# Hybrid encoder layer on one core: whole loads at the start, two steps in halves at the end, and a token tile finished by a transfer

## The chip, the core and the metric

The kernel runs on one core of a Trainium2 chip. The core has TensorE (matmuls; PE in the profile, its weight loads PEld), VectorE (DVE), ScalarE (ACT), GpSimd (POOL) and SyncE (SP), which work side by side and wait for each other by semaphores. Transfers between HBM and the on-chip memory are issued from SP, ACT or POOL and move by 16 DMA engines. POOL can also issue a transfer that adds what it carries to what stands at its destination. The metric is the device time of the kernel in microseconds.

## The reference

One layer of a hybrid streaming encoder in fp32, batch 1, 512 tokens, model width 1024, recurrent width 1280, 16 attention heads, feed-forward width 3072:

```python
h = rms_norm(x, mix_norm_pre)
proj = h @ w_in                       # -> xa, ga, q, k, v, f_logit, g_a, g_b
xc = causal_dwconv(xa, conv_a_w, conv_a_b)
hr = rg_lru(xc, w_rg_a, b_rg_a, w_rg_x, b_rg_x, lru_lambda)
y_a = gelu(ga) * hr
y_b = forgetting_attention(q, k, v, f_logit + b_forget)
merged = sigmoid(g_a + b_merge[0]) * (y_a @ w_proj_a) + sigmoid(g_b + b_merge[1]) * (y_b @ w_proj_b)
x = x + rms_norm(merged @ w_out, mix_norm_post)
h = rms_norm(x, ffn_norm_pre)
up = causal_dwconv(h @ w_up, conv_f_w, conv_f_b)
gate, val = split(up)
x = x + rms_norm((gelu(gate) * val) @ w_down, ffn_norm_post)
```

`rms_norm` divides a token's row by the root of its mean square and multiplies by a gain. So nothing of a token can be scaled before its whole row of 1024 is there.

## The kernel before, in words

Every product is made of three matmuls: each fp32 operand is split into a high and a low part, and high by high, high by low and low by high are summed in a PSUM bank. The high part is a cast on ScalarE (`wh`, `hh`, `ah`; line 172 for a weight), the low part a subtraction, mostly on VectorE (`wl`, line 175). A weight tile is 128x1024 fp32, 512 KB, and comes by a transfer on SP's queue (`raw`, line 166). In part of the stages the weight's low part is made without VectorE: ScalarE writes minus the high part (line 361), and POOL issues a transfer that adds the raw weight to it (line 362).

The stages follow each other on TensorE: the norm of x and the first four `xa` units (to about 36 us), the rest of the input projection with the recurrent branch (to 235), the two merge gates `ma` and `mb` (235 to 335), attention (to 480), the projections and `wo` (to 540), the second norm and the first `up` units (to 590), the `up` units in pairs (to 790), and the `down` product with the last norm.

The order within each stage is partly written out by hand (`manual_schedule`: instructions stand on an engine in the order of the code), partly set by the framework's scheduler, which may move an instruction where its inputs and buffers allow; `issue_after` holds an instruction behind another one.

The prologue (lines 557 to 676) is written out by hand. x comes in four token tiles of 128 tokens (`xt`), tiles 0 and 1 in halves of 512 columns. For each tile ScalarE makes the sum of squares (`sumsq` by halves with an addition on VectorE for tiles 0 and 1, `sumsq_whole` for 2 and 3) and the root, VectorE the reciprocal (`rs`) and the scaling by the gain (`scaled`, line 616), TensorE turns the 128x128 blocks (`turn`, line 245), ScalarE casts the result into `hh` (`evac_hi`, line 249), and VectorE makes `hl` (`evac_lo`). The gain is first spread over all partitions by four matmuls against ones (line 595). `spin(n)` are n matmuls whose result nobody reads, in the bank of `xa3`. `X` is the first half of the 512 tokens (tiles 0 and 1), `Y` the second. The first four `xa` units are done in halves, X of all four and then Y of all four (`half`, which issues 24 matmuls of 256 columns).

The gates and the `up` pairs use a Strassen-like scheme (`Halved`, `Pair`): two units share seven products of sums of quarters. `period` runs a pair `p` together with the finishing of the pair before it and the preparation of the two behind. The parts that need a plain weight quarter come by `plain_low` and `plain_high`, in index 0 for a whole tile (128x1024) and index 1 for half a tile.

The second norm (`mix_norm`, a generator that is run in pieces) makes `x2t`, the residual stream, and its scaled rows `xn`, which are turned (`tr_f`, line 260) for the `up` product. While tiles 2 and 3 of it are under way, TensorE does the first halves of some `up` units (`first_half`), and `fetch` loads and splits the weights ahead of them.

The `down` product has seven products of six steps each (`STEPS`), into banks `dn`. The last one is product 2, for token tiles 0 and 1; its last four steps (`LATE`) are held back and run per token tile, tile 1 in two column halves with a bank each, so that the norm of the first half can begin early. At the end `fold_part` adds the bank into `kept` and squares it, `gained_part` multiplies by the gain, `scale_of` makes the reciprocal root (`rs_o`), and the result is finished in one of two ways:

```python
def finish(t, c, queue):
    dve.scalar_tensor_tensor(out=os[t][:, c], in0=os[t][:, c], scalar=rso[t], in1=x2t[:, t, c],
                             op0=ALU.mult, op1=ALU.add)
    queue.dma_start(ov[:, t, c], os[t][:, c])

def finish_by_dma(t, queue):
    act.activation(out=os[t], in_=os[t], func=AF.Copy, scale=rso[t])
    nc.gpsimd.dma_start(os[t], x2t[:, t], accum_op=ALU.add)
    queue.dma_start(ov[:, t], os[t])
```

Tiles 2 and 3, which are ready while TensorE still works, take `finish_by_dma` (2 with its store on POOL, 3 on SP). Tiles 0 and 1 take `finish`.

Of the kernel before, what the change touches and what calls it, by code (L numbers as in the profile page):

```python
# [63 lines left out]
def kernel(  # L64
# [267 lines left out]
    class Halved:  # L332


        def __init__(self, prefix, block, xh, xl):
            self.prefix, self.block, self.xh, self.xl = prefix, block, xh, xl
            self.sh = self.sl = self.tpool = self.kpool = self.stpools = None

    class Pair:


        def __init__(self, st, j, tiles):
# [4 lines left out]
            self.w, self.t, self.th, self.x, self.ml = {}, {}, {}, {}, {}  # L347

# [18 lines left out]
        def plain_high(self, i):  # L367
# [75 lines left out]
    def period(p, b, n1, n2, epilogue, load):  # L443
# [22 lines left out]
        n2.plain_low(0)  # L466
# [19 lines left out]
    with ExitStack() as rg:  # L486
        rt, ixt, tt = {}, {}, {}
        last_act = [None]
        with ExitStack() as r0:
# [68 lines left out]
            with tc.tile_pool(name="pre", bufs=2, side="right", reuse_waits="tile") as pre, ExitStack() as wp:  # L558
                offset(wp, 256, "right")
                wpre = wp.enter_context(tc.tile_pool(name="wpre", bufs=3, side="right", reuse_waits="tile"))  # L560
# [14 lines left out]
                us += [Split(*order[t][1:], order[t][0], (wpre, None)[t - 2]) for t in range(2, NF)]  # L575
# [14 lines left out]
                for i, c in enumerate(HALVES):  # L590
# [8 lines left out]
                def sumsq(t):  # L599
                    xns[t] = pre.tile([P, D], F32, tag="xn", name=f"xn{t}")  # L600
                    s2 = small.tile([P, 2], F32, tag="s2", name=f"s2_p{t}")
                    for i, c in enumerate(HALVES):
                        act.activation(out=xns[t][:, c], in_=xts[t][:, c], func=AF.Square, accum_out=s2[:, i : i + 1])
                    ss = small.tile([P, 1], F32, tag="ss", name=f"ss_p{t}")
                    dve.tensor_tensor(out=ss, in0=s2[:, 0:1], in1=s2[:, 1:2], op=ALU.add)
                    rss[t] = rstd_of(ss, f"p{t}")
# [24 lines left out]
                sumsq(0)  # L631
# [18 lines left out]
                wh, wl = us[0].parts()  # L650
                for w, h in ((wh, hh), (wh, hl), (wl, hh)):
                    for k in range(KD):
                        pe.matmul(pss[0][:, X], w[:, k], h[:, k, X], start=w is wh and h is hh and k == 0, stop=w is wl and k == KD - 1)
# [7 lines left out]
                scaled(3, 1)  # L661
                us[2].hi()
# [250 lines left out]
    with ExitStack() as g2:  # L913
# [14 lines left out]
        gates.stpools = [st0pool, st1pool]  # L928
        none = Nothing()
# [239 lines left out]
    turned = {}  # L1169
    with ExitStack() as mix:  # L1170
# [12 lines left out]
        def mix_norm(t, acc):  # L1183
# [21 lines left out]
            for c in HALVES:  # L1205
                dve.scalar_tensor_tensor(out=xn[:, c], in0=x2t[:, t, c], scalar=rs, in1=gb[1][:, c],
                                         op0=ALU.mult, op1=ALU.mult)
# [60 lines left out]
        fetch(where[f"up{1 + JF}"])  # L1268
        first_half(1)
        next(g2)  # L1270
        next(g3)
# [125 lines left out]
    wd, yraw, yhl, dpools, LATE = {}, {}, {}, [], 4  # L1397
# [339 lines left out]
```

## Time and profile before

| what | value |
|---|---|
| median of the three runs shown | 912.75 us (912.56 to 912.94) |
| profiled execution, device time | 912.11 us |
| its span (first to last instruction) | 910.3 us |
| granted clock of TensorE, mean | 0.998 |
| TensorE busy | 900.5 us |
| VectorE, ScalarE, POOL busy | 728.1, 601.6, 219.5 us |
| moved by transfers | 187.86 MB, mean 206 GB/s |

The profile belongs to one execution. Its device time is 1.8 us longer than its span, and differences between two kernels are taken between like numbers. A row of a timeline reads: start in us, duration, engine, line, operation, output <- inputs, shapes, how many instructions, and in brackets the idle time ahead of it with the engine, tile and line that ended it. A row of the chain has the start, the duration and what carried it. Matmuls overlap: one of 256 columns is listed with 0.28 us, but they start 0.12 us apart, and the step from start to start is its price.

### The profile page before, as it was taken

Reading aid. Unit: us, or ns where it says so; the run is one execution under the profiler, and the core shown is the slowest. Engines: PE = TensorE matmul, PEld = TensorE weight load, DVE = VectorE, ACT = ScalarE, POOL = GpSimd, SP = SyncE. Lnnn points to the kernel's source line nnn. Section 1 sums busy time; section 2 is a strip of 40 time slices with the busy share of each in tenths; the row PEclk is TensorE's granted clock in tenths of the full one; section 3 lists DMA queues with packets and bytes.
Section 4 is the critical chain, followed back from the end, with each engine's and each line's share of the span. In section 5 each row is a group of like instructions: output and inputs, shape, how many; then the busy total and the mean of one; then the engine's idle time right before and its main releaser. Section 6 shows DMA issues by size and latency. Waiting matters only on the chain.

```text
span 910.3 us, 15947 instructions
## 1 busy us (share of the span) xinstructions
PE 900.5 (99%) x5906; PEld 803.4 (88%) x5906; DVE 728.1 (80%) x1201; ACT 601.6 (66%) x1041; POOL 219.5 (24%) x281
## 2 busy tenths in 40 slices
PE   8999999999999999999999999999999999999997
PEld 7988888878899998888888889999999999988886
DVE  6966369638777649888778588989999999889897
ACT  7555495433367748776654487878888888677664
POOL 4134345544111112212104100233323223100000
PEclk9999999999999999999999999999999999999999
DMA  8767589989967877434415654478988988699774
GB/s 287 243 206 210 166 200 257 277 218 187 208 162 187 208 240 261 167 130 165 156 66 172 209 182 144 118 179 203 238 214 212 242 198 218 208 398 330 241 202 147
DMA packets 72048, 187.86 MB, mean 206 GB/s; under 512 B 7265, under 2 KB 27793, under 8 KB 71586
## 3 DMA queue, kind: packets, MB, share of 16 engines
q1 hardware_dynamic: 47648, 127.72, 42.2%
q0 software_dynamic: 24176, 58.99, 30.5%
q8 instruction: 46, 0.75, 0.3%
q14 instruction: 32, 0.26, 0.1%
q10 hardware_dynamic: 146, 0.14, 0.0%
HBM read 150.69 MB, written 35.73 MB: 205 GB/s over the span
## 4 chain that ended last, share of the span: by engine, by line
PE 97%; ACT 1%; DVE 1%; DMA 1%; issue 0%; SPq 0%; DVEq 0%; ACTq 0%
PE up L418 7%; PE up L419 7%; PE up L421 7%; PE dn L1446 4%; PE dn L1445 4%; PE dn L1444 4%; PE ga L219 2%; PE ga L217 2%; PE pa L219 2%; PE pa L218 2%; PE pa L217 2%; PE ga L218 2%; PE k L217 2%; PE q L217 2%; PE pb L217 2%; PE k L219 2%
## 5 line engine op out<-in xcount | busy, mean ns | idle before, releaser
L1321 DVE SCALAR_TENSOR_TENSOR u<-up,cpt,u 128x511 f32<-128x511 f32 x96 | 71.3, 745 | 3.5 <-ACT u L1315 1.8
L362 POOL DMA_DIRECT2D ml<-raw_up x41 | 35.3, 862 | 152.9 <-ACT ml L361 89.4
L1446 PE MATMUL dn<-wh_dn,al 128*128 128x512 f32 (+1 forms) x180 | 67.6, 375 | 0.0
L1445 PE MATMUL dn<-wl_dn,ah 128*128 128x512 f32 (+1 forms) x180 | 67.5, 375 | 0.0
L1444 PE MATMUL dn<-wh_dn,ah 128*128 128x512 f32 (+1 forms) x180 | 67.5, 375 | 0.0
L418 PE MATMUL up<-sh,th 128*128 128x256 f32 x252 | 60.2, 276 | 0.0
L419 PE MATMUL up<-sl,th 128*128 128x256 f32 x252 | 60.2, 276 | 0.0
L175 DVE TENSOR_TENSOR wl_dn<-raw_dn,wh_dn 128x1024 fp32r<-128x1024 f32 x42 | 51.2, 1220 | 9.5 <-ACT wh_dn L172 9.3
L172 ACT CAST wh_dn<-raw_dn 128x1024 fp32r<-128x1024 f32 x42 | 44.1, 1050 | 20.3 <-issue 6.9
L1315 ACT ACTIVATE u<-up,cpt 128x512 f32<-128x512 f32 x48 | 36.9, 778 | 21.6 <-PE up L421 11.7
L324 DVE TENSOR_TENSOR tl<-t,th 128x1024 fp32r<-128x1024 f32 x42 | 51.0, 1217 | 0.0
L419 PEld LDWEIGHTS up<-sl,th 128*128 128x128 f32 x252 | 47.3, 188 | 0.0
L418 PEld LDWEIGHTS up<-sh,th 128*128 128x128 f32 x252 | 47.3, 188 | 0.0
L1329 POOL TENSOR_TENSOR yf<-u,u 128x512 f32<-128x512 f32 x23 | 31.4, 1367 | 63.1 <-issue 48.5
L400 ACT CAST th<-t 128x1024 fp32r<-128x1024 f32 x42 | 43.8, 1044 | 3.1 <-DVE t L324 0.6
L418 PE MATMUL up<-h2h,mh 128*128 128x256 f32 x168 | 40.2, 276 | 0.0
L419 PE MATMUL up<-h2l,mh 128*128 128x256 f32 x168 | 40.2, 276 | 0.0
L1446 PEld LDWEIGHTS dn<-wh_dn,al 128*128 128x128 f32 x180 | 33.9, 188 | 6.3 <-DVE al L324 0.2
L1445 PEld LDWEIGHTS dn<-wl_dn,ah 128*128 128x128 f32 x180 | 33.9, 188 | 6.1
L1444 PEld LDWEIGHTS dn<-wh_dn,ah 128*128 128x128 f32 x180 | 33.9, 188 | 6.0
L421 PE MATMUL up<-sh,tl 128*128 128x256 f32 x252 | 38.8, 276 | 0.0
L1005 ACT ACTIVATE P<-P,mx 128x384 f32<-128x384 f32 (+3 forms) x64 | 35.2, 553 | 4.2 <-DVE mx L1000 3.3
(727 smaller groups left out, 3231.0 us busy)
## 6 DMA issues: line engine op xcount, KB each, us to landing
raw_up<-in_w_up_dram SPq DMA_DIRECT2D x48, 512.0 KB, 5.3
td<-in_w_down_dram POOLq DMA_DIRECT2D x36, 512.0 KB, 7.1
raw_dn<-td SPq DMA_DIRECT2D x24, 512.0 KB, 5.2
B<-cnd POOLq DMA_DIRECT2D x16, 640.0 KB, 5.4
ml<-raw_up POOLq DMA_DIRECT2D x20, 512.0 KB, 5.2
raw_dn<-in_w_down_dram SPq DMA_DIRECT2D x18, 512.0 KB, 4.4
raw_wo<-in_w_out_dram SPq DMA_DIRECT2D x16, 512.0 KB, 3.7
td<-td POOLq DMA_DIRECT2D x12, 512.0 KB, 12.6
```

Source lines behind the costliest of these rows:

```text
L172: act.copy(self.wh, self.raw)
L175: engine.tensor_tensor(out=self.wl, in0=self.raw, in1=self.wh.bitcast(F32), op=ALU.subtract)
L217: pe.matmul(dst, ah, bh, start=first, stop=False)
L219: pe.matmul(dst, al, bh, start=False, stop=last)
L324: dve.tensor_tensor(out=out, in0=a, in1=b, op=ALU.subtract)
L418: pe.matmul(dst, wh[:, k], ah[:, k], start=first and k == 0, stop=False, skip_group_check=True)
L419: pe.matmul(dst, wh[:, k], al[:, k], start=False, stop=False, skip_group_check=True)
L421: pe.matmul(dst, wl[:, k], ah[:, k], start=False, stop=k == KH - 1, skip_group_check=True)
L1321: dve.scalar_tensor_tensor(out=c[:, s:], in0=ps[:, : S - s], scalar=col(C_CFW + 3 * e + j), in1=c[:, s:], op0=ALU.mult, op1=ALU.add)
L1444: pe.matmul(d[:, x], ah[:, k, tok], wh[:, k, x], start=first, stop=False, skip_group_check=True)
L1445: pe.matmul(d[:, x], ah[:, k, tok], wl[:, k, x], start=False, stop=False, skip_group_check=True)
L1446: pe.matmul(d[:, x], al[:, k, tok], wh[:, k, x], start=False, stop=last, skip_group_check=True)
```

## The change

There are five parts.

1. **Prologue.** Tiles 0 and 1 of x are loaded whole, and their squares are made whole. The spins are spread between the gain matmuls. On ScalarE the cast of the first weight comes ahead of the evacuations of tile 0. After the X halves of `xa0` and `xa1`, all turns of tiles 2 and 3 follow, then the Y halves of both; `xa2` and `xa3` are done in 512 columns. `wpre` has two buffers, and units 2 and 3 take theirs from the general pool.
2. **Gates.** With `gates.subtract`, `period` doesn't call `plain_low(0)`; the low part of a whole tile is subtracted on VectorE, a little later (`plain_rest`).
3. **First up units.** The fetch for the second unit of pair 1 comes after `first_half(1)`, and its low parts are held behind `xn` of tile 2.
4. **Last steps.** Of tile 1's product 2, only the last two steps (`SPLIT`) are in column halves, into two banks of their own; the steps ahead of them go in 512 columns into a third bank, which is folded separately.
5. **Tile 0** is finished by `finish_by_dma`, with its store on POOL.

```diff
-    def fetch(i):
+    def fetch(i, last=None):
...
             w.hi()
-            w.lo(dve)
+            with tc.issue_after(last.ins) if last else ExitStack():
+                w.lo(dve)
...
+        def plain_rest(self):
+            if self.left:
+                sub(*self.left)
+                self.left = None
+
-        def plain_high(self, i):
+        def plain_high(self, i, low=True):
...
                 l = self.split_tile(i, "ml")
-                sub(l, src, h.bitcast(F32))
+                if low:
+                    sub(l, src, h.bitcast(F32))
+                else:
+                    self.left = l, src, h.bitcast(F32)
...
-        n2.plain_low(0)
+        if not p.st.subtract:
+            n2.plain_low(0)
...
-        n2.plain_high(0)
+        n2.plain_high(0, not p.st.subtract)
         n1.p12()
         if b:
             n1.sums_lo(1)
+        n2.plain_rest()
...
-                wpre = wp.enter_context(tc.tile_pool(name="wpre", bufs=3, side="right", reuse_waits="tile"))
+                wpre = wp.enter_context(tc.tile_pool(name="wpre", bufs=2, side="right", reuse_waits="tile"))
...
                 for t in range(2):
-                    for c in HALVES:
-                        nc.sync.dma_start(xts[t][:, c], xv[:, t, c])
+                    nc.sync.dma_start(xts[t], xv[:, t])
...
                         pe.matmul(pgain[i], one, g, start=j == 0, stop=j == 1)
+                        spin(2 - i)
...
+                def by_kind(i, c, kinds):
+                    wh, wl = us[i].parts()
+                    for n, (w, h, k0, k1) in enumerate(kinds):
+                        for k in range(k0, k1):
+                            pe.matmul(pss[i][:, c], (wh, wl)[w][:, k], (hh, hl)[h][:, k, c],
+                                      start=n == 0 and k == k0, stop=n == len(kinds) - 1 and k == k1 - 1)
+
+                spin(1)
+                sumsq_whole(0)
                 scaled(0, 0)
                 scaled(0, 1)
                 turn(0, 0)
                 turn(0, 1)
-                spin(3)
-                sumsq(1)
+                sumsq_whole(1)
+                us[0].hi()
+                us[0].lo(pool)
                 evac_hi(0, 0)
                 evac_hi(0, 1)
-                us[0].hi()
-                us[0].lo(pool)
...
+                half(1, X)
+                for g in range(2):
+                    for t in (2, 3):
+                        turn(t, g)
+                for g in range(2):
+                    for t in (2, 3):
+                        evac_hi(t, g)
+                        evac_lo(t, g)
...
-                half(1, X)
+                by_kind(0, Y, ((0, 0, 0, KH), (1, 0, 0, KH), (0, 0, KH, KD), (1, 0, KH, KD), (0, 1, 0, KD)))
+                half(1, Y)
                 for t in (2, 3):
-                    for g in range(2):
-                        turn(t, g)
-                        evac_hi(t, g)
-                        evac_lo(t, g)
-                half(2, X)
-                half(3, X)
-                for t in range(NF):
-                    half(t, Y)
+                    project(pss[t], us[t].parts(), hh, hl)
...
+        gates.subtract = True
...
             for c in HALVES:
-                dve.scalar_tensor_tensor(out=xn[:, c], in0=x2t[:, t, c], scalar=rs, in1=gb[1][:, c],
-                                         op0=ALU.mult, op1=ALU.mult)
+                scaled2[t] = dve.scalar_tensor_tensor(out=xn[:, c], in0=x2t[:, t, c], scalar=rs, in1=gb[1][:, c],
+                                                      op0=ALU.mult, op1=ALU.mult)
...
-        fetch(where[f"up{1 + JF}"])
         first_half(1)
         next(g2)
+        fetch(where[f"up{1 + JF}"], scaled2[2])
...
-                slot[n][1] = [slot[n][1], bank("dn2_2")]
+                slot[n][1] = [slot[n][1], *(bank(f"dn2_1{x}") for x in "xy")]
...
+            m0 = 0
             if isinstance(dst[t], list):
-                outs = [(dst[t][h], x) for h, x in enumerate((X, Y)) if c in (None, x)]
+                whole, *parts = dst[t]
+                m0 = 0 if m < NS - SPLIT else NS - SPLIT
+                outs = [(d, x) for d, x in zip(parts, (X, Y)) if c == x] if m0 else [(whole, slice(0, DH))]
...
-        late_steps((0,))
-        late_steps((1,), X)
-        late_steps((1,), Y)
+        late_steps(LATE, 0, (0,))
+        late_steps(LATE, SPLIT, (1,))
+        late_steps(SPLIT, 0, (1,), X)
+        late_steps(SPLIT, 0, (1,), Y)
...
         scale_of(0)
+        finish_by_dma(0, nc.gpsimd)
+        fold(1, 1, slot[2][1][0])
         fold_part(1, X, 0)
-        finish(0, HALVES[1], nc.sync)
         gained_part(1, X)
-        finish(0, HALVES[0], nc.sync)
```

The order of the instructions shows three places. The first is ScalarE at the start. `xn<-xt` is the sum of squares, `sd_p` the root, `hh` the evacuation of a turned block, `wh_xa` the weight cast. Before:

```order
L603 ACTIVATE xn_195,s_p_196<-xt_144 128x512 x2
L236 ACTIVATE sd_p_201<-ss_p_199,epst 128x1
L603 ACTIVATE xn_220,s_p_221<-xt_145 128x512 x2
L236 ACTIVATE sd_p_226<-ss_p_224,epst 128x1
L249 CAST hh<-tr_p_0_207 128x4x128
L249 CAST hh<-tr_p_1_212 128x4x128
L172 CAST wh_xa_153<-raw_xa_152 128x1024
L249 CAST hh<-tr_p_0_235 128x4x128
L249 CAST hh<-tr_p_1_241 128x4x128
```

And ScalarE at the same place now:

```order
L615 ACTIVATE xn_200,ss_p_201<-xt_144 128x1024
L237 ACTIVATE sd_p_203<-ss_p_201,epst 128x1
L615 ACTIVATE xn_219,ss_p_220<-xt_145 128x1024
L237 ACTIVATE sd_p_222<-ss_p_220,epst 128x1
L172 CAST wh_xa_151<-raw_xa_150 128x1024
L250 CAST hh<-tr_p_0_209 128x4x128
L250 CAST hh<-tr_p_1_214 128x4x128
L250 CAST hh<-tr_p_0_231 128x4x128
L250 CAST hh<-tr_p_1_237 128x4x128
```

The squares are whole, and the weight cast has moved ahead of the evacuations of tile 0.

The second place is VectorE around the second norm of tiles 2 and 3 (`u`, `x2t`, `ss`, `rs` and `xn` are steps of the norm; `wl_up` are the low parts of weights). Before:

```order
L175 TENSOR_TENSOR wl_up_6379<-raw_up_6377,wh_up_6378 128x1024
L1189 TENSOR_TENSOR u_6285<-wo_0_6021,gain_5860 128x512
L1189 TENSOR_TENSOR u_6285<-wo_1_6022,gain_5860 128x512
L1192 TENSOR_TENSOR ss_mix_6355<-s_mix_6287 128x1
L175 TENSOR_TENSOR wl_up_6450<-raw_up_6448,wh_up_6449 128x1024
L1189 TENSOR_TENSOR u_6292<-wo_0_6023,gain_5860 128x512
L1189 TENSOR_TENSOR u_6292<-wo_1_6024,gain_5860 128x512
L238 RECIPROCAL rs_mix_6359<-sd_mix_6357 128x1
L1192 TENSOR_TENSOR ss_mix_6361<-s_mix_6294 128x1
L175 TENSOR_TENSOR wl_up_6505<-raw_up_6503,wh_up_6504 128x1024
L238 RECIPROCAL rs_mix_6365<-sd_mix_6363 128x1
L1198 SCALAR_TENSOR_TENSOR x2t<-u_6285,rs_mix_6359,x2t 128x512 x2
```

And VectorE now, from the end of tile 2's norm on:

```order
L1214 TENSOR_TENSOR ss_f_6344<-s_f_6309 128x1
L1214 TENSOR_TENSOR ss_f_6358<-s_f_6314 128x1
L239 RECIPROCAL rs_f_6348<-sd_f_6346 128x1
L1217 SCALAR_TENSOR_TENSOR xn_2_6228<-x2t,rs_f_6348,gain_5803 128x512 x2
L175 TENSOR_TENSOR wl_up_6354<-raw_up_6352,wh_up_6353 128x1024
L239 RECIPROCAL rs_f_6362<-sd_f_6360 128x1
L175 TENSOR_TENSOR wl_up_6392<-raw_up_6390,wh_up_6391 128x1024
L1217 SCALAR_TENSOR_TENSOR xn_3_6235<-x2t,rs_f_6362,gain_5803 128x512 x2
L266 TENSOR_TENSOR h2l<-tr_f_0_6366,h2h 128x8x64
L266 TENSOR_TENSOR h2l<-tr_f_1_6367,h2h 128x8x64
L175 TENSOR_TENSOR wl_up_6447<-raw_up_6445,wh_up_6446 128x1024
```

Three subtractions of weights that stood between the steps of the norm stand behind `xn` of tile 2: two of them ahead of `xn` of tile 3, one behind it.

The third place is POOL at the end (`o<-x2t` is the adding transfer, `out_dram<-o` a store; `o_9774`, `o_9775` are tiles 2 and 3). Before:

```order
L1330 DMA yd_6796<-yf_9750 128x512
L1578 DMA o_9774<-x2t 128x1024
L1579 DMA out_dram<-o_9774 128x1024
L1578 DMA o_9775<-x2t 128x1024
L1733 UNCONDITIONAL_BRANCH
```

And POOL now, where `o_9716`, `o_9717` are tiles 2 and 3 and `o_9714` is tile 0:

```order
L1341 DMA yd_6738<-yf_9692 128x512
L1592 DMA o_9716<-x2t 128x1024
L1593 DMA out_dram<-o_9716 128x1024
L1592 DMA o_9717<-x2t 128x1024
L1592 DMA o_9714<-x2t 128x1024
L1593 DMA out_dram<-o_9714 128x1024
L1748 UNCONDITIONAL_BRANCH
```

Two transfers for tile 0 are added as POOL's last instructions; the two stores of tile 0 are gone from SP.

More of the change, by code (lines that the diff above doesn't have):

```diff
@@ L574 @@
                     nc.sync.dma_start(xts[t], xv[:, t])
-                us += [Split(*order[t][1:], order[t][0], (wpre, None)[t - 2]) for t in range(2, NF)]
+                us += [Split(*order[t][1:], order[t][0]) for t in range(2, NF)]
                 nc.sync.dma_start(cpt, cp)
@@ L595 @@
                         pe.matmul(pgain[i], one, g, start=j == 0, stop=j == 1)
+                        spin(2 - i)
                 xns, rss, ptr, lasts = {}, {}, {}, [None, None]
[L599 to L606, printed above, removed]
                 def sumsq_whole(t):
@@ L649 @@
                     evac_lo(1, g)
[L650 to L653, printed above, removed]
+                by_kind(0, X, ((0, 0, 0, KD), (0, 1, 0, KD), (1, 0, 0, KD)))
                 us[1].hi()
@@ L1624, with late_steps @@
                 f()
-        def late_steps(ts, c=None):
-            for i in range(len(STEPS) - LATE, len(STEPS)):
+        def late_steps(n0, n1, ts, c=None):
+            for i in range(len(STEPS) - n0, len(STEPS) - n1):
                 down_step(i, ts, c)
-        late_steps((0,))
-        late_steps((1,), X)
-        late_steps((1,), Y)
+        late_steps(LATE, 0, (0,))
+        late_steps(LATE, SPLIT, (1,))
+        late_steps(SPLIT, 0, (1,), X)
+        late_steps(SPLIT, 0, (1,), Y)
         def fold_part(t, c, i):
-            dve.tensor_tensor(out=kept[1][t][:, c], in0=slot[2][t][c.start // SH][:, c] if t else slot[2][t], in1=kept[1][t][:, c], op=ALU.add)
+            dve.tensor_tensor(out=kept[1][t][:, c], in0=slot[2][t][1 + c.start // SH][:, c] if t else slot[2][t], in1=kept[1][t][:, c], op=ALU.add)
             act.activation(out=junk[:, c], in_=kept[1][t][:, c], func=AF.Square, accum_out=s2o[t][:, i : i + 1])
```

9 lines of the change are left out of this document (5 added, 4 removed).

## The prediction

> **What bounds the kernel now.** I read the page's busy totals first, then its chain by engine, then the waits of TensorE, and then the chain in order of time at the two ends of the run.
>
> ```profile
> PE 900.5 (99%) x5906; PEld 803.4 (88%) x5906; DVE 728.1 (80%) x1201; ACT 601.6 (66%) x1041; POOL 219.5 (24%) x281
> PE 97%; ACT 1%; DVE 1%; DMA 1%; issue 0%; SPq 0%; DVEq 0%; ACTq 0%
> PE tr_f L260 <- DVE xn L1206: 0.5, 1, 0.5
> ```
>
> TensorE is busy for 900.5 of 910.3 us, and the chain lies on it for 97%. A change can therefore do three things: shorten TensorE's own work, close one of its few holes, or alter the two ends, where TensorE is not the bound. The only wait behind the start that the view lists is the 0.5 us for `xn`. Start and end in order of time:
>
> ```profile
> 2.13 5.36 DMA xt<-in_x_dram
> 7.51 0.73 ACT xn L603 x2
> 8.76 0.96 ACT hh L249 x2
> 9.72 0.95 ACT wh_xa L172
> 10.66 0.50 ACT hh L249
> 11.20 3.32 PE xa L653 x24
> 14.52 0.12 PE xa L229
> 17.35 1.75 PE tr_p L245 x16
> ...
> 897.80 0.23 PE dn L1446
> 898.38 0.12 PE dn L1444
> 903.66 0.13 PE dn L1446
> 906.80 0.40 DVE o L1572
> ```
>
> Columns are start, duration, and what carried the chain. At the start everything waits for the second half of token tile 1 of x (5.36 us under way), then for ScalarE, and the first useful matmul begins at 11.20. From there TensorE runs on. At the end it stops at 903.66 + 0.13 = 903.79; the norm of tile 1 ends at 907.20, and its last store and the finish take the span to 910.30.
>
> **The change part by part.** The profiled execution took 912.11 us, of which the span is 910.3; the median of the runs shown, 912.75, is 0.64 above it. I sum against 912.11 and add 0.64 at the end.
>
> *Start.* The view of ScalarE and the moved bytes of the first 12 us (40 slices of 0.3 us):
>
> ```profile
> 3.46 0.63 ACT L603 ACTIVATE xn<-xt 128x512 f32<-128x512 f32 x1 [0.66 <-DMA xt<-in_x_dram]
> 12.57 1.06 ACT L611 ACTIVATE xn<-xt 128x1024 f32<-128x1024 f32 x1
> GB/s 0 0 0 0 0 41 123 232 410 348 389 294 280 328 225 225 307 335 382 335 362 362 396 403 423 410 410 382 410 437 423 396 410 437 423 410 423 423 423 423
> ```
>
> Two loads of whole tiles replace four of halves. Summing the slices, the first megabyte (tiles 0 and 1) has gone through by about 5.1 us, yet tile 1's second half counts as landed at 2.13 + 5.36 = 7.49. Some of its packets were overtaken. If two larger loads pass in order, tile 1 lands near 5.4. No row shows such a load at this place, so the bounds are 5.1 and 7.5. I take 5.4, because the bytes are the harder evidence.
>
> ScalarE then does the square of tile 1 in one piece (1.06, and 0.2 for reading the sum: 5.4 to 6.6) and its root (to 6.9). Then come the weight cast, which now stands ahead of the four evacuations, and those: 0.95 + 0.96 + about 1.0 (the two of tile 1; the second of them is the 0.50 row), so 9.8. With 0.2 of gaps the first product begins at 10.0 rather than 11.20: 1.2 gained. Landing at 7.5 gives 7.5 + 1.25 + 0.3 + 2.9 = 11.95, less about 0.3 where the evacuations of tile 0 wait for nothing: 0.45 lost. Landing at 5.1 and a TensorE already at its quick pace gives 9.5: 1.7 gained. The interleaved spins cost nothing, as TensorE has nothing else there.
>
> Then units 2 and 3 take 512 columns at once. A half unit is 24 matmuls in 17.35 - 14.52 = 2.83 (0.118 each); 512 columns cost 0.227 (897.80 row). So 96 x 0.118 - 48 x 0.227 = 11.33 - 10.90 = 0.43 gained, as TensorE has no gap there. Start in all: 1.6 (0 to 2.1).
>
> *Gates.* Six pairs replace a ScalarE copy of 128x1024 and an accumulating transfer of 512 KB by a VectorE subtraction.
>
> ```profile
> 271.60:281.20 9.60, 9.60 (x85) 9.60 (x85) 7.22 (x12) 7.08 (x12) 1.72 (x2) 1.00 0.82 211
> L361 ACT ACTIVATE gml<-raw_mb x8: 636/844/1053, 283.7 to 317.0; 128x1024 fp32r<-128x1024 f32 x4, 128x512 fp32r<-128x512 f32 x4
> L324 DVE TENSOR_TENSOR gml<-raw_ma,gmh x2: 684/955/1226, 255.1 to 256.2; 128x1024 fp32r<-128x1024 f32 x1, 128x512 fp32r<-128x512 f32 x1
> 294.74 0.28 PE L419 MATMUL mb<-hl,gmh 128*128 128x256 f32 x1
> 294.96 0.74 PE L421 MATMUL mb<-hh,gml 128*128 128x256 f32 x4
> ```
>
> A period lasts 9.6 us, with VectorE busy 7.22 and ScalarE 7.08 (third and fourth number after the span). The 1.22 of a 128x1024 subtraction brings VectorE to 8.4: it still fits. ScalarE falls by 1.05. Both are beside TensorE, so they cost nothing; without that cover, six times 1.22 is 7.3. TensorE's step from 294.74 to 294.96 is 0.22 where 0.12 is usual: the `gml` transfer was just late. That goes: 0.1. Bounds -0.3 (a late subtraction or two) and +0.2; I take 0.1.
>
> *First up units.* Three weight subtractions of 1.22 leave their place ahead of the second norm's last tiles and come behind `xn_2`.
>
> ```profile
> 552.47 1.23 DVE L175 TENSOR_TENSOR wl_up<-raw_up,wh_up 128x1024 fp32r<-128x1024 f32 x1
> 554.94 1.22 DVE L175 TENSOR_TENSOR wl_up<-raw_up,wh_up 128x1024 fp32r<-128x1024 f32 x1
> 560.33 1.41 DVE L1206 SCALAR_TENSOR_TENSOR xn<-x2t,rs_f,gain 128x512 f32<-128x512 f32 x2
> 559.71 1.07 PE L232 MATMUL up<-h2h,wl_up 128*128 128x256 f32 x8
> 561.23 1.03 PE L260 MATMUL tr_f<-ident,xn 64*128 64x64 f32 x16 [0.45 <-DVE xn L1206]
> 566.00:582.00 16.00, 16.00 (x143) 16.00 (x143) 15.90 (x24) 13.01 (x20) 1.78 (x2) 1.00 0.30 84
> ```
>
> TensorE's eight matmuls from 559.71 step by 0.11, so the last starts at 560.51; the transposes start at 561.23, 0.6 late, and wait within their group once more, an estimated 0.3, for the second half of `xn` (done at 560.33 + 1.41 = 561.74). With the two rows of 552.47 and 554.94 gone from before it, `xn` can come 2.4 earlier at most, and 0.9 closes the hole. What is late next: the moved subtractions. VectorE is busy 15.90 of 16 us behind it, so their 3.7 us are worked off late there, and TensorE, 0.9 earlier, asks sooner. Bounds: 0 (the hole reappears some us later) and 0.9; I take 0.6, since TensorE itself shows no gap in that row, which leaves some margin.
>
> *Down product, last steps.* For tile 1, 48 half matmuls become 24 whole ones: 48 x 0.12 - 24 x 0.227 = 0.3 of TensorE. This moves only tile 1's tail. VectorE gains one fold of 512 columns there and loses two multiply-adds of as many, so it isn't later. Tile 1 then ends near 906.9.
>
> *Tile 0 by transfer.* VectorE's multiply-adds and two stores go. In their place ScalarE scales 128x1024, POOL issues a transfer that adds `x2t` into `o`, and behind its landing another that stores. Tiles 2 and 3 do this already:
>
> ```profile
> 901.10 0.17 DVE L238 RECIPROCAL rs_o<-sd_o 128x1 f32<-128x1 f32 x1 [0.36 <-ACT sd_o L236]
> 883.07 1.15 ACT L1577 ACTIVATE o<-o,rs_o 128x1024 f32<-128x1024 f32 x1 [0.29 <-DVE rs_o L238]
> 896.46 1.15 ACT L1577 ACTIVATE o<-o,rs_o 128x1024 f32<-128x1024 f32 x1 [0.23 <-DVE rs_o L238]
> 884.52 0.86 POOL L1578 DMA_DIRECT2D o<-x2t  x1 [83.08 <-ACT o L1577]
> 889.50 0.56 POOL L1579 DMA_DIRECT2D out_dram<-o  x1 [4.12 <-DMA o<-x2t]
> 898.67 0.85 POOL L1578 DMA_DIRECT2D o<-x2t  x1 [8.60 <-ACT junk L1558]
> 903.22 0.34 SPq L1579 DMA_DIRECT2D out_dram<-o  x1
> out_dram<-o POOLq DMA_DIRECT2D x1, 512.0 KB, 3.8
> out_dram<-o SPq DMA_DIRECT2D x1, 512.0 KB, 2.7
> out_dram<-o SPq DMA_DIRECT2D x1, 128.0 KB, 2.0
> ```
>
> Tile 0's scale is there at 901.27, so ScalarE ends at 901.30 + 1.15 = 902.45. Then, by tile 2: 0.30 to the issue (884.22 to 884.52), 4.98 to the store's issue, 3.8 to its landing: 911.5. By tile 3: 1.06 to the issue (897.61 to 898.67), 4.55, and 3.8: 911.9. I take 911.7. The last landing today is tile 1's store: 907.20 + 2.0 = 909.2, and the span ends 1.1 behind it. So the tail grows by 2.5. Bounds: a store in an idle machine at SyncE's 2.7 and an addition a little quicker than both rows, at 4.0, give 902.45 + 0.3 + 4.0 + 0.3 + 2.7 = 909.75, or +0.6; both transfers at 5.2 with the late issue give 902.45 + 1.06 + 5.2 + 0.3 + 5.2 = 914.2, or +5.0. VectorE's saved multiply-adds bring nothing, as tile 1's tail is no longer the last.
>
> The Trainium skill ("DMA: Bandwidth & Descriptors", section "Anatomy of one DMA — SWDGE (gpsimd) path") fits 2.0 us plus the bytes over 436 GB/s, an estimate of 3.2 us for 512 KB. The rows here, 4.55 to 4.98 from issue to issue and 3.8, are slower. By the page the two would land at 902.45 + 0.3 + 3.2 + 0.3 + 3.2 = 909.45, and the tail would grow by 0.25 instead of 2.5.
>
> *Sum.* -1.6 (start) - 0.1 (gates) - 0.6 (up) + 2.5 (end) = +0.2. Profiled execution 912.3, median 912.95, say 912.9.
>
> **Rivals.**
>
> *The transfers of tile 0 are nearly hidden.* For it: the two rows of tiles 2 and 3 were taken while weights were loading, and this is the end. Against it: the store of tile 3 runs beside it from 903.22. Tail +0.6: -1.7 in sum, 911.0. It counts as faster from a tail of +0.5. The page's 3.2 us is of this kind.
>
> *The transfers of tile 0 come late (the other side).* One mechanism: POOL's queue serves them at 5.2 us each behind the late issue, because tile 3's store shares the engines. Tail +5.0, sum +2.7, 915.4. It decides from a tail of +4.1, that is a last landing behind 913.3. For it speaks the 0.76 by which tile 3's issue came later than tile 2's; against it, that no such transfer near the end took over 5.
>
> *The start gains nothing.* Tile 1 lands at 7.5 as before: the start gives 0, the sum is +1.8, 914.5. For it: the late packets may come from the loads queued behind, which stay. Against it: the byte sum.
>
> *VectorE falls behind in the up units*, the hole only moves, and the gates lose a little: sum +1.1, 913.9.
>
> *The stages in front don't pass their gain on*, because a weight load now comes last: at most the 1.6 of the start is lost. TensorE waits for no load behind 12 us but the `gml` one, so this has little for it; it ends near the third rival.
>
> **How the numbers follow.** Forecast 0.55 (tail +1.5 to +3.8, start 1 to 2: 911.6 to 914.4), hidden transfers 0.15, late transfers 0.10, no start gain 0.12, VectorE behind 0.08. I call 0.2% (1.8 us) what a measurement can tell from no change. Faster (below 910.9): most of the hidden case where the start reaches its upper bound, 0.14. Slower (above 914.6): the late case, half of the no-gain case, and a rest of the forecast, 0.19. Within: 0.67. The range for 8 in 10 is 911.0 to 915.0; it reaches to the hidden case below and nearly to the late one above.
>
> **What would show it.** Start: the first `xa` product near 10.0, `xt` landing near 5.4, units 2 and 3 with 512 columns. Gates: no 512 KB `gml` transfer on POOL in those periods, TensorE without a gap at 294. Up: no step over 0.2 us at `tr_f`, nor in the 30 us behind. End: the chain's last piece is the store of tile 0 on POOL, with `o<-x2t` issued near 902.8 and the store near 907.4 (both less what the front has gained). I am wrong if the chain still ends with tile 1, if the first product begins behind 11, or if TensorE has new gaps between 250 and 335 or 560 and 600.

## The result and the profile after

The changed kernel takes 918.41 us (median, 918.12 to 920.17), the kernel before 912.65 on the same chip: a ratio of 1.0066, 95% interval 1.0051 to 1.008. It is 5.8 us slower. The forecast was 912.9, in a range from 911.0 to 915.0.

The page of the changed kernel, with the busy totals and the chain by engine:

```profile
PE 903.6 (99%) x5842; PEld 802.6 (88%) x5842; DVE 737.1 (80%) x1204; ACT 596.4 (65%) x1032; POOL 216.5 (24%) x277
PE 89%; DVE 5%; issue 3%; ACT 2%; DMA 1%; POOL 0%; POOLq 0%; DVEq 0%; ACTq 0%
```

TensorE is no longer the chain nearly to the end: its share fell from 97% to 89%, VectorE's rose from 1% to 5%, and "issue" (time in which the engine waited for nothing that the profile shows) rose from 0% to 3%. To find where the 6.1 us of span went, I set the same matmuls of the two traces side by side (start times in us):

| matmul | before | after | later by |
|---|---|---|---|
| first `xa` product | 11.20 | 13.87 | 2.67 |
| first `v` | 81.62 | 83.93 | 2.31 |
| last `mb` | 348.98 | 351.21 | 2.23 |
| last `wo` | 552.13 | 554.20 | 2.07 |
| first pair product of `up` | 590.44 | 591.67 | 1.23 |
| last `up` | 791.34 | 793.50 | 2.16 |
| last `dn` | 903.50 | 905.34 | 1.84 |
| end of the span | 910.33 | 916.46 | 6.13 |

(The last few `mb` matmuls run as late as that, among those of attention.) So there are two losses: about 2.7 ahead of the first product, and 4.3 behind the last matmul. In the middle the `up` stage gains 0.8 and gives 0.9 back, units 2 and 3 give 0.4, and the down product 0.3.

**The start.** The chain of the changed kernel in order of time, then the rows of ScalarE and VectorE that tell why:

```profile
3.57 0.72 PE gain L607
4.29 1.15 PE xa L596 x4
...
8.76 0.72 PE gain L607
9.48 1.15 PE xa L596 x4
10.63 3.24 PE tr_p L246 x16
13.88 3.30 PE xa L639 x24
```

```profile
4.30 1.06 ACT L615 ACTIVATE xn<-xt 128x1024 f32<-128x1024 f32 x1 [1.50 <-DMA xt<-in_x_dram]
5.68 1.04 ACT L615 ACTIVATE xn<-xt 128x1024 f32<-128x1024 f32 x1
9.52 0.75 DVE L620 SCALAR_TENSOR_TENSOR xn<-xt,rs_p,gain 128x512 f32<-128x512 f32 x1 [2.57 <-PE gain L607]
```

The load did what was forecast: tile 1 landed at 5.53, and when ScalarE gets to it at 5.68 its row names no wait. But the chain now runs over TensorE from 3.57 on. Behind each gain matmul (0.72) stand spins (1.15 for two of them, recorded as x4), the next gain matmul stands behind these, and the last one begins at 8.69 where it began at 4.95. VectorE needs the gain to scale the rows: it waits 2.57 us for it, and the second half of tile 0 is scaled at 9.52. The turns of both tiles then follow the last spins, from 10.43 on.

**The up units.**

```profile
583.85 2.79 ACT L1326 ACTIVATE u<-up,cpt 128x512 f32<-128x512 f32 x4 [0.64 <-DVE sl L1262]
590.29 2.35 DVE L325 TENSOR_TENSOR tl<-t,th 128x1024 fp32r<-128x1024 f32 x2
593.18 0.43 DVE L448 TENSOR_TENSOR up<-up,x 128x256 f32<-128x256 f32 x1 [0.54 <-ACT x L436]
593.67 0.38 PE L429 MATMUL up<-sh,th 128*128 128x256 f32 x1 [0.48 <-DVE up L448]
```

The hole at the turns of the second norm is closed: the waits of TensorE no longer list `tr_f`. In its place TensorE waits 0.48 at 593 for an addition on VectorE, and from the first pair product to the last `up` matmul it takes 201.83 us instead of 200.90. The addition itself waits 0.54 for a copy on ScalarE, and ScalarE had waited 0.64 for VectorE at 583.85. In the kernel before, that copy still had to wait for TensorE, but only for 0.20:

```profile
590.64 0.37 ACT L425 COPY x<-up 128x256 f32<-128x256 f32 x1 [0.20 <-PE up L421]
```

**The end.**

```profile
904.94 0.86 POOL L1592 DMA_DIRECT2D o<-x2t  x1 [3.98 <-ACT o L1591]
910.27 0.56 POOL L1593 DMA_DIRECT2D out_dram<-o  x1 [4.47 <-DMA o<-x2t]
out_dram<-o POOLq DMA_DIRECT2D x1, 512.0 KB, 2.9
910.25 0.59 POOLq L1748
```

The store of tile 0 is issued at 910.27 and lands 2.9 later, at 913.16. The span doesn't end 1.1 behind that, as before, but 3.3. The views above don't count the instruction that fills this time; the trace's own records do. At the end of each engine's program stands a DRAIN, and POOL's is long:

```
            POOL's last    its last transfer   POOL's drain   SP's waits   span
            issue ends     landed              ends           end          ends
before        899.52            903.13            905.71         909.6     910.3
after         910.84            913.16            915.68         913.9     916.5
```

Before, POOL's drain was over 3.9 us ahead of SP's waits. Now it ends 4.85 behind the end of the store's issue, 1.8 behind SP's waits, and everyone waits for it. In both kernels it ends 2.5 to 2.6 behind the landing of POOL's last transfer.

### The profile page after: what moved, and what is told of

It reads as the page before. It is cut to its first block, busy times and chain, and to the rows that moved or that the text cites. A ratio compares the mean times of both kernels' runs of the same rounds, so it can differ in the third digit from the quotient of the medians.

```text
span 916.5 us, 15794 instructions
## 1 busy us (share of the span) xinstructions
PE 903.6 (99%) x5842; PEld 802.6 (88%) x5842; DVE 737.1 (80%) x1204; ACT 596.4 (65%) x1032; POOL 216.5 (24%) x277
## 4 chain that ended last, share of the span: by engine, by line
PE 89%; DVE 5%; issue 3%; ACT 2%; DMA 1%; POOL 0%; POOLq 0%; DVEq 0%; ACTq 0%
PE up L429 7%; PE up L430 7%; PE up L432 7%; PE dn L1460 2%; PE dn L1458 2%; PE dn L1459 2%; PE pa L218 2%; PE ga L220 2%; PE ga L218 2%; PE pa L219 2%; PE pa L220 2%; PE ga L219 2%; PE k L218 2%; PE q L218 2%; PE pb L218 2%
## 5 line engine op out<-in xcount | busy, mean ns | idle before, releaser
L1460 PE MATMUL dn<-wh_dn,al 128*128 128x512 f32 x164 | 63.9, 390 | 0.0
L1458 PE MATMUL dn<-wh_dn,ah 128*128 128x512 f32 x164 | 63.8, 389 | 0.0
L1459 PE MATMUL dn<-wl_dn,ah 128*128 128x512 f32 x164 | 63.8, 389 | 0.0
L1460 PEld LDWEIGHTS dn<-wh_dn,al 128*128 128x128 f32 x164 | 30.8, 188 | 6.6 <-DVE al L325 0.3
L448 DVE TENSOR_TENSOR up<-up,x 128x256 f32<-128x256 f32 x63 | 27.2, 432 | 11.6 <-PE up L432 9.2
L1459 PEld LDWEIGHTS dn<-wl_dn,ah 128*128 128x128 f32 x164 | 30.8, 188 | 6.4
## 6 DMA issues: line engine op xcount, KB each, us to landing
td<-td POOLq DMA_DIRECT2D x12, 512.0 KB, 10.7
```

Of the source, the lines that this page charges most:

```text
L1458: pe.matmul(d[:, x], ah[:, k, tok], wh[:, k, x], start=first, stop=False, skip_group_check=True)
L1459: pe.matmul(d[:, x], ah[:, k, tok], wl[:, k, x], start=False, stop=False, skip_group_check=True)
L1460: pe.matmul(d[:, x], al[:, k, tok], wh[:, k, x], start=False, stop=last, skip_group_check=True)
```

## The experiments

Each ran beside the kernel before; the ratios are to that. "Theory A" is the spins, "theory B" POOL's drain, "theory D" the moved subtractions of the `up` units; R1 to R8 are the rivals that the expectations name.

### The spins as before

```diff
-                        spin(2 - i)
...
-                spin(1)
                 sumsq_whole(0)
...
                 turn(0, 1)
+                spin(3)
                 sumsq_whole(1)
```

> The changed kernel with the spins as before: none between the gain matmuls, three behind the turns of tile 0. All else of the change stays. Theory A (the spins between the gain matmuls hold the gain, and with it the scaling and the turns): the last gain matmul ends near 5.4 instead of 9.4, the first xa product begins at 10.0 to 11.0 instead of 13.9, and the time falls by 2.9 to 3.9, to 914.5 to 915.5. Rival R1 (the whole loads, the whole squares or the cast ahead of the evacuations are what costs): the first product stays behind 13, time 917.5 to 918.5.

Measured: 916.62 us, ratio 1.0037 (1.0025 to 1.005). Rows of TensorE:

```profile
4.94 0.62 PE L607 MATMUL gain<-gain_xl,one 1*128 1x512 f32 x1
7.05 1.94 PE L246 MATMUL tr_p<-ident,xn 128*128 128x128 f32 x8 [1.49 <-ACT xn L614]
8.78 1.49 PE L596 MATMUL xa<-ident 128*128 128x128 f32 x6
10.06 1.91 PE L246 MATMUL tr_p<-ident,xn 128*128 128x128 f32 x8
11.80 1.76 PE L638 MATMUL xa<-hh,wh_xa 128*128 128x256 f32 x8
```

The gain is done at 5.4 again and the first product begins 2.1 earlier, which A said and R1 denied. But it is 11.8, not 10 to 11: the three spins that used to fill a wait for tile 1 now stand, from 8.78 to 10.06, in front of turns that were ready. The time, too, missed A's 914.5 to 915.5.

### The kernel before with only the new spins

```diff
                         pe.matmul(pgain[i], one, g, start=j == 0, stop=j == 1)
+                        spin(2 - i)
...
+                spin(1)
                 sumsq(0)
...
-                spin(3)
```

> The kernel before with only the spins of the change. Theory A: the second half of the gain comes at 9.5, the turns of tile 0 end behind 11, the first product begins near 14 instead of 11.2, the time grows by 2.5 to 3.5, to about 915.5. R1: the spins are in the shadow of the late load of tile 1, which this kernel still has; no more than 0.5 later, 912.7 to 913.2.

Measured: 915.9 us, ratio 1.0032 (1.0021 to 1.0042), and in its profile:

```profile
9.52 0.75 DVE L617 SCALAR_TENSOR_TENSOR xn<-xt,rs_p,gain 128x512 f32<-128x512 f32 x1 [2.58 <-PE gain L595]
14.45 0.74 PE L654 MATMUL xa<-hh,wh_xa 128*128 128x256 f32 x4 [0.84 <-ACT hh L249]
```

There is the same wait of 2.6 for the gain, and a first product at 14.45. The spins alone cost the kernel before 2.9 us (0.0032 x 912.7). That settles A from the other side.

### No spins but the first four

```diff
-                        spin(2 - i)
...
-                spin(1)
```

> The changed kernel with the four spins at the very start only: none between the gain matmuls and none behind the turns of tile 0. Beside the run with the old spins, in which the turns of tile 1 stood behind three spins until 10.1 although their input was ready near 8.4. Theory A: the turns of tile 1 start at 8.8, the first product begins at 10.5 to 11.0 instead of 11.8, and the time is 0.8 to 1.3 below that run, 915.3 to 915.8. Rival R6 (the spins are needed to bring TensorE to its quick pace): the matmuls stay at 0.21 a step beyond 13, and the gain is under 0.3, 916.3 to 916.9.

Measured: 915.58 us, ratio 1.0032 (1.0019 to 1.0045).

```profile
6.98 3.49 PE L246 MATMUL tr_p<-ident,xn 128*128 128x128 f32 x16 [1.42 <-DVE xn L619]
10.45 1.43 PE L638 MATMUL xa<-hh,wh_xa 128*128 128x256 f32 x8
PE ma L429 <- DVE ma L448: 0.3, 1, 0.3
PE mb L429 <- DVE mb L448: 0.2, 1, 0.2
```

The first product begins at 10.45 and the time is 915.58, as A said, and the quick pace is there by 10.7: R6 falls. The first `v` comes at 80.52, 1.1 earlier than before the change. In this execution, which took 916.69, part of that is lost again: TensorE waits for `ma` and `mb` additions in the gates, and by the last `wo` it is 0.35 ahead (551.78 against 552.13).

### The store of tile 0 on SP

```diff
-        finish_by_dma(0, nc.gpsimd)
+        finish_by_dma(0, nc.sync)
```

> The changed kernel with the store of token tile 0 issued from SP instead of POOL; the adding transfer stays on POOL. Theory B (POOL's closing drain lasts 5 to 7 us behind its last transfer, longer than the store itself, and the kernel ends with it): the drain starts behind the adding transfer at 905.8 and is over by 912, the span ends about 1.1 behind the landing, 2.0 to 2.3 earlier: 916.1 to 916.4. Rival R2 (what is long is the landing of the last store, whoever issues it): 918.0 to 918.4.

Measured: 917.17 us, ratio 1.0043 (1.0029 to 1.0057). This run decides less than it was meant to. POOL's drain was over at 912.8 and not the last, as B said; but the store, which waits for the addition, stood in SP's queue ahead of tile 1's stores:

```profile
905.08 5.74 SPq L1593 DMA_DIRECT2D out_dram<-o  x2
910.87 1.19 SPq L1588 DMA_DIRECT2D out_dram<-o  x2
```

Tile 1's stores were issued from 910.87 on instead of 908.3, behind 512 KB, and the new last landing ate half of the gain.

### The store of tile 0 last on SP

```diff
-        finish_by_dma(0, nc.gpsimd)
+        act.activation(out=os[0], in_=os[0], func=AF.Copy, scale=rso[0])
+        nc.gpsimd.dma_start(os[0], x2t[:, 0], accum_op=ALU.add)
...
         finish(1, Y, nc.sync)
+        nc.sync.dma_start(ov[:, 0], os[0])
```

> The changed kernel with the store of tile 0 as the very last transfer on SP, behind those of tile 1, where it holds up nobody; the adding transfer stays on POOL. Theory B: the store is issued when the adding transfer has landed (near 910.3 to 910.8) and lands 2.7 later; POOL's drain begins behind the adding transfer at 905 and is over by 912.8, so the span ends 1.1 behind the landing, 914.3 to 914.8, which is 1.7 to 2.2 below the changed kernel: 916.2 to 916.7. Rival R2 (the end is late by the landing alone, whoever stores): 918.0 or more.

Measured: 916.0 us, ratio 1.0034 (1.0022 to 1.0047). POOL's drain ended at 912.29, SP's waits at 913.2, the span at 913.95: the landing is the last again, and the tail behind TensorE is 8.7 instead of 11.1 us. The store landed at 912.61, 0.55 earlier than from POOL, and the span ended 2.5 earlier. So the landing explains about a fifth of the gain and the drain the rest: B holds, R2 falls.

### One small store on POOL, in the kernel before

```diff
-        finish(1, X, act)
+        finish(1, X, nc.gpsimd)
```

> The kernel before with one store moved: the 128 KB store of the first half of tile 1's last columns is issued from POOL instead of ScalarE, at the same place (near 906.8). Nothing else differs, and the store lands at about 909 either way. Theory B (a drain of 5 to 7 us on POOL follows its last transfer and holds the end): the drain runs from 906.8 to 911.8 or later, the span ends about 0.6 behind it, near 912.5 to 914, and the time grows by 2 to 4, to 914.7 to 916.7. Rival R4 (the long drain belongs to the large adding transfers): no more than 0.4 slower, 912.7 to 913.1.

Measured: 915.29 us, ratio 1.0024 (1.0014 to 1.0034).

```profile
907.10 0.58 POOL L1574 DMA_DIRECT2D out_dram<-o  x1 [7.58 <-DVE o L1572]
out_dram<-o POOLq DMA_DIRECT2D x1, 128.0 KB, 2.3
907.08 0.60 POOLq L1733
```

The store has landed by 909.4 and SP is through at 909.8, but POOL's drain ends at 911.98 and the span at 912.8. The drain is therefore not a matter of 512 KB or of adding transfers (R4): it ends 4.3 behind the issue of a 128 KB store, which is 2.6 behind its landing, as in the other traces.

### Tile 0 finished on VectorE

```diff
-        finish_by_dma(0, nc.gpsimd)
...
         fold_part(1, X, 0)
+        finish(0, HALVES[1], nc.sync)
         gained_part(1, X)
+        finish(0, HALVES[0], nc.sync)
```

> The changed kernel with token tile 0 finished as before, by two multiply-adds on VectorE and two stores on SP. Theory B with the tail as read from the trace: tile 1 is the last again, the span ends 4.0 to 4.4 earlier, 914.0 to 914.4. Rival R3 (the end is late because of the last steps and the extra fold, not of tile 0): less than 1 is gained, 917.5 to 918.4.

Measured: 914.57 us, ratio 1.0024 (1.0016 to 1.0033), 3.8 us below the changed kernel, so R3 falls. Tile 1 is the last again. The tail is 7.4 us, 0.6 more than before the change, and this is why:

```profile
905.58 0.75 DVE L1586 SCALAR_TENSOR_TENSOR o<-o,rs_o,x2t 128x512 f32<-128x512 f32 x1
906.24 0.42 DVE L1649 TENSOR_TENSOR kept<-dn_1y,kept 128x256 f32<-128x256 f32 x1
```

The second multiply-add of tile 0 holds the last fold, for which TensorE's matmuls were done; in the changed kernel that fold ran at 905.65. With only two steps in halves, the second half follows the first sooner, and VectorE has no room for both multiply-adds between them.

### The fetch at its old place

```diff
+        fetch(where[f"up{1 + JF}"])
         first_half(1)
         next(g2)
-        fetch(where[f"up{1 + JF}"], scaled2[2])
```

> The changed kernel with the fetch of the up weights at its old place. Theory D (the hole at the turns is closed, but VectorE's moved subtractions come due at the first pair, where TensorE waits 0.9): the hole of 0.9 at the turns is back, the waits near 593 to 595 are gone, and the time stays within 0.3 of the changed kernel, 918.1 to 918.7. Rival R5 (what TensorE lost near 593 has to do with the later start, not with the moved subtractions): the hole comes back and the waits near 593 stay, 919.0 to 919.5.

Measured: 918.46 us, ratio 1.0061 (1.0047 to 1.0076). From the last `wo` to the first pair product TensorE takes 37.95 instead of 37.47 us, and for the rest of `up` 200.92 instead of 201.83; no wait for VectorE is left near 593, and ScalarE's wait of 0.64 is gone. What the fetch gains in one place it gives back in the other, as D said. R5 falls. (The hole at the turns was smaller here, about 0.5.)

### The prologue alone, without its new spins

The kernel before with the changed lines 570 to 683, less `spin(2 - i)` and `spin(1)`.

> The kernel before with the changed prologue alone and without its added spins: whole loads and squares, the cast first, units 2 and 3 in 512 columns. Theory A: the first product begins near 10.45 instead of 11.2 and the half units save 0.4, so TensorE is 1.1 earlier from 80 us on, and the time falls by 0.9 to 1.2, to about 911.5. Rival R7 (a weight load or VectorE takes the gain back in the gates or the up units): TensorE is 1.1 earlier at 80 us but not at 550, and the time is 912.2 to 912.9.

Measured: 912.59 us, ratio 0.9994 (0.9984 to 1.0004): no difference, the time that R7 expected. The profiled execution took 913.75, so it doesn't show the median. In it the first weight landed at 8.54, where six of the other nine traces with both tiles whole have it at 6.8 to 6.9, and ScalarE waited for it:

```profile
8.56 1.05 ACT L172 CAST wh_xa<-raw_xa 128x1024 fp32r<-128x1024 f32 x1 [1.19 <-DMA raw_xa<-in_w_in_dram]
PE xa L638 <- ACT hh L250: 0.3, 1, 0.3
PE ma L429 <- DVE ma L448: 0.3, 1, 0.3
```

The first product began at 11.12, at the slow pace until 12.96, and the gates lost 0.9 on top. That isn't R7's way, for TensorE had no lead to lose: the first `v` came at 81.73, 0.1 later than before the change. No trace shows whether other executions have the forecast gain; the lowest time, 911.27, is 0.3 below the lowest of the kernel before (911.6).

### Tile 0 finished by POOL's own addition

```diff
-                        spin(2 - i)
...
-                spin(1)
...
-        finish_by_dma(0, nc.gpsimd)
+        act.activation(out=os[0], in_=os[0], func=AF.Copy, scale=rso[0])
+        for c in HALVES:
+            pool.tensor_tensor(out=os[0][:, c], in0=os[0][:, c], in1=x2t[:, 0, c], op=ALU.add)
+            nc.sync.dma_start(ov[:, 0, c], os[0][:, c])
```

> The changed kernel with four spins only, and token tile 0 finished without a transfer on POOL's queue: ScalarE scales it as in the change, POOL itself adds the residual in two halves, and two stores go out on SP. Against the run without spins (915.6): the tail from TensorE's last matmul falls from 11.8 to 6.8 us, the last to land is tile 1's store again, and the time falls by 4.6 to 5.0, to 910.6 to 911.0, below the kernel before. Rival R8 (POOL's two additions slow VectorE's chain for tile 1 or come late themselves): the tail stays above 8, 912 or more.

Measured: 912.6 us, ratio 0.9995 (0.9985 to 1.0006). With the two causes gone the loss is gone: the ratio went from 1.0066 to 1.0032 without the spins and to 0.9995 without the transfers as well. A gain isn't there, and the time is the one that R8 expected. In the trace TensorE's last matmul is 1.25 earlier than before the change (902.25 against 903.50), and the tail takes 1.0 of that back. It is 7.8 us, between the two expectations:

```profile
901.63 2.94 POOL L1658 TENSOR_TENSOR o<-o,x2t 128x512 f32<-128x512 f32 x2 [3.77 <-ACT o L1656]
905.55 0.40 DVE o L1584
```

VectorE's chain isn't held (R8's first half falls), and SP was through at 908.4. POOL's drain, which now follows two additions and no transfer, ended at 909.3 and the span at 910.1: 0.9 of tail are the drain even here.

### The same with tile 0 of x in halves

```diff
-                for t in range(2):
-                    nc.sync.dma_start(xts[t], xv[:, t])
+                for c in HALVES:
+                    nc.sync.dma_start(xts[0][:, c], xv[:, 0, c])
+                nc.sync.dma_start(xts[1], xv[:, 1])
...
-                sumsq_whole(0)
+                sumsq(0)
```

> The run before in this list with token tile 0 of x loaded and squared in halves, as in the kernel before, and tile 1 whole. If the whole load of tile 0 is what made its square start at 4.3 instead of 3.5, the chain of tile 0 is 0.5 to 0.8 earlier, the first product begins near 9.9, and the time falls by 0.4 to 0.6. If tile 1, which lands near 5.7, sets the start (its square follows that of tile 0 on ScalarE), nothing is gained: within 0.2.

Measured: 914.28 us, ratio 1.0017 (1.0007 to 1.0026), 1.7 slower than the run above.

```profile
3.50 0.63 ACT L616 ACTIVATE xn<-xt 128x512 f32<-128x512 f32 x1 [0.70 <-DMA xt<-in_x_dram]
6.67 1.06 ACT L624 ACTIVATE xn<-xt 128x1024 f32<-128x1024 f32 x1 [1.02 <-DMA xt<-in_x_dram]
```

Tile 0 is earlier by 0.9, as expected, but tile 1 landed at 6.64, against 5.53 to 5.77 in the ten traces with both tiles whole. Neither expectation foresaw a loss. The first product is 0.55 later (11.08 against 10.53), but at the first `v` only 0.1 of that is left (80.88 against 80.77). The profiled execution took 912.86, well below the median, so most of the 1.7 stays open.

### The same with gates and fetch as before

The run with POOL's addition, without `gates.subtract` and with the fetch at its old place.

> The second run of this list with the gates and the fetch of the up weights as before, so that the start and the end alone are changed. Theory D says the fetch gives 0.8 and takes 0.9, and the gates 0.1 to 0.2: within 0.4 of that run. If the subtractions on VectorE are what makes TensorE wait 0.5 at 261 and 0.4 at 329 in the run without spins, the time falls by 0.5 to 0.9.

Measured: 912.53 us, ratio 0.9993 (0.9982 to 1.0003): the same as with both. Together the two parts can't be told from nothing. TensorE still has a step of 0.27 at 329.47, where 0.12 is usual, so the subtractions are not what costs there.

## Why the prediction was wrong, point by point

**What bounds the kernel** was read rightly: TensorE in the middle, the two ends as the places where time is made or lost. Both losses are at the ends.

**Start: wrong, and the largest miss.** The step that failed is "The interleaved spins cost nothing, as TensorE has nothing else there." TensorE had nothing else, but the gain matmuls stood behind the spins in its order, VectorE's scaling behind the gain, and the turns behind both. The spins were costed by TensorE's idle time, not by who waits for what is queued behind them. Forecast 1.6 gained, measured 2.3 lost; adding the spins to the kernel before cost 2.9 us, taking them out of the changed one gave 3.1 (1.0066 to 1.0032). The terms beside it were nearer: tile 1 landed at 5.53 (forecast 5.4), units 2 and 3 gave 0.36 (0.43), and without the spins the first product came at 10.45 (10.0). Missing there was that a whole load holds tile 0's square until 4.30 where the half began it at 3.46. Yet even without the spins the prologue alone didn't move the median, which is the third rival's result, though not by its late tile 1. The four traces of the changed prologue without spins have the first `v` at 80.52, 80.77, 81.19 and 81.73, against 81.62 before. The last of them had the late weight, and in the two late ones TensorE kept its slow pace until 12.4 and 12.9; in the others it ended at 10.2 and 11.0.

**Gates: right within what can be seen.** The 0.2 step at 294.74 is gone, but it is also missing in the run with one store on POOL, which has the old gates, so it belonged to one execution. From the first `v` to the last `mb` nine traces with the changed gates took 267.0 to 268.3 us and five with the old ones 267.1 to 268.3.

**First up units: wrong by 0.7, at its lower bound.** "0 (the hole reappears some us later)" is what happened, at 593 instead of 561: 0.84 gained, 0.93 given back. I had taken 0.6 because TensorE showed no gap there before. That it had no gap told nothing of the margin, which was the 0.20 for which ScalarE's copy waited; VectorE's late work reached TensorE by way of ScalarE.

**Down product:** 0.3 forecast, 0.32 measured.

**Tile 0 by transfer: right in its direction and up to the landing, wrong behind it.** Relative to the start of the down product the store landed at 913.16 - 2.16 = 911.0, forecast 911.7; the addition took 5.3 from issue to issue (rows: 4.55 and 4.98), the store 2.9 (row: 3.8). The Trainium skill's fit ("DMA: Bandwidth & Descriptors", section "Anatomy of one DMA — SWDGE (gpsimd) path", an estimate of 3.2 us for 512 KB) is near the store here and too short for the addition. The term that failed is "the span ends 1.1 behind it". That was read from an end at which POOL had long been done; behind a transfer of POOL's the end is the drain, and the span ended 3.3 behind the landing, 2.2 us more. The forecast of +2.5 for the tail became +4.0 (6.13 less the 2.16 by which the down product starts later).

**The rivals.** The one on the other side named the right place, tile 0's transfers, but a wrong mechanism: the addition did take 5.0 to its landing, but the store took 2.9, and the issue was not late, only 0.29 behind ScalarE. That its tail of +4.0 nearly reached the +4.1 of this rival is luck. VectorE falling behind in the up units happened, without the loss in the gates. Of the chances, 0.19 for slower was too little, mainly because the spins had no rival at all.

## What to carry to other kernels

Filler work on an in-order engine is free only if nothing that others wait for stands behind it: before calling it free, follow its queue to the next instruction with a reader. An end at which another engine was last says nothing of what an engine's own end costs, so a transfer or even an addition put last on POOL has to be priced with POOL's drain: here the landing and 2.5 us more before the others go on. A moved step gains only if the engine it lands on is ahead at the later place too, and an absence of waits doesn't show that it is.

## What the runs showed of the hardware that was not expected

- **POOL's drain.** In the eleven traces in which a transfer is POOL's last work, the drain ends 2.3 to 2.6 us behind the landing of that transfer: 2.58 behind an adding one in the kernel before, 2.52 behind the 512 KB store in the changed one, 2.62 behind the 128 KB store. No run was made to test this. Where two plain additions were POOL's last work, it ended 2.9 to 4.7 behind them; what sets that stays open.
- **TensorE's pace.** A matmul step of 128 columns is 0.21 us at first and 0.11 later. The profile's rows print a granted clock of 1.00 for the whole start, but the trace holds no clock record ahead of the change of pace: the first one begins at 9.30 in the kernel before and at 13.57 in the changed one, where the steps shorten. In the six traces with spins between the gain matmuls it begins at 12.5 to 14.6, in the eight without them at 9.3 to 13.0. So these spins brought the quick pace no earlier, although TensorE was never idle from 1.5 on. The Trainium skill ("TensorE: Matmul & The Clock Gate", section "Part 1: The HAM clock gate (the "warmup" mystery)") tells of a free-running window of about 3.4 us that has to be busy. Counted from the first turn, or from the spins behind the last gain matmul, the change came 2.8 to 6.0 us later here, which is of that size, though the shortest is below it; whether a matmul over one row counts as busy no run here isolates.
- **Order of loads.** In the one execution with loads of x in 2 KB rows ahead of one in 4 KB rows, that one landed about 0.9 to 1.1 later (6.64 against 5.53 to 5.77).
